# LoRA forward on one core: 12 projecting matmuls of 512 columns for 24 of 256, and a spread in two instructions a quadrant

## The chip, the cores and the metric

The kernel runs on one core of a Trainium2 chip. A core has five engines with instruction streams of their own: TensorE (PE, matmuls; its weight loads are shown apart as PEld), VectorE (DVE), ScalarE (ACT), GpSimd (POOL) and SyncE (SP), which issues the transfers here. Sixteen DMA engines move data between the chip's memory and the core's SBUF. Matmuls write into PSUM, a second memory. Engines order their work by semaphores. The metric is the time of one execution on the device, in microseconds (us); the kernel before takes 123.55 us (median of three runs, 123.49 to 123.74).

## The reference

```python
x      # 16 x 512 x 768, float32: 8192 tokens of 768
A      # 768 x 16;  B: 16 x 768;  scale = 0.5
lora = np.matmul(np.matmul(x, A), B)
return (x + scale * lora).astype(np.float32)
```

Every token is projected from 768 values to 16 (y = x A), raised back to 768 (y B), halved and added to x. x and the result are 25 MB each.

## The kernel before

**Tiles and groups.** The 8192 tokens are 64 tiles of 128 tokens, one token a partition. They lie in five parts of 9, 7, 16, 16 and 16 tiles (PARTS). SBUF holds 48 tiles of x as float32 (x_sb); the last part takes the place of the first two, once those are stored. Work goes in 8 groups of 8 tiles (GROUP); a group is raised and summed in four pairs of tiles.

**One group, step by step.**

1. Narrowing (L194): ScalarE copies the first four tiles and GpSimd the last four from x_sb (float32) to xn (float16). For groups after the first they wait for s_taken, which says that the projection of the group before has started and xn is free.
2. Turning (L250): VectorE transposes xn into xt in blocks of 32 x 32. It takes pairs of float16 values for one float32, so a block turns 32 tokens against 32 pairs. In xt a partition holds, for its quadrant of 32 tokens, one pair of columns of x out of each of 12 stretches of 64 columns (NC = 12); the two halves of a pair lie next to each other along the free axis (index k).
3. Projecting (L281): 24 matmuls of 256 columns (8 tiles x 32 tokens), one for each stretch c and half k, add up in ps_yt. The moving operand takes every second float16 of xt. The stationary operand w_bd[:, c, k, :] is block diagonal: quadrant b of the partitions holds the 32 rows of A of that stretch and half, in columns 32 b to 32 b + 15; the other 16 columns of each quadrant are zero. The last of the 24 raises s_y.
4. Spreading (L238): four instructions of ScalarE, one a quadrant, scale ps_yt by 0.5 and write it as float16 to the diagonal blocks of y_bd. What lies off the diagonal was set to zero once. The fourth raises s_spread.
5. Raising (L302): for each pair, four matmuls (512, 256, 256 and 512 columns) of y_bd with b_mm into one of two PSUM buffers (lora_ps). b_mm holds B four times, 32 partitions apart, with zeros in the other rows.
6. Summing (L255): VectorE adds lora_ps to x_sb, in place, one instruction a pair.

**The order of the work.** It is written out by hand for each engine. TensorE, for each group: raise pairs 0 and 1, wait for the next group's turning, the first half of its projection, raise pairs 2 and 3, the second half of the projection. Pair 0 waits for s_spread, each pair for a free buffer (s_free). VectorE: turn group g + 1, then sum the four pairs of group g. ScalarE: narrow group g + 1, then spread group g.

**The transfers.** All are issued by SP in one order: loads of the first two parts with A and B between, the loads of parts 2 and 3, stores 0 and 1 (16 tiles in all), loads 6 and 7 (8 tiles each, into the place of what was stored, each after one of these stores has landed), and stores 2, 3 and 4 (16 tiles each). A store waits for the sums of its tiles (s_sum). Two have one more gate: stores 0 and 1 wait for s_lora (L169), the second raised pair of group 2, and store 2 waits for s_raise (L181), the first raising matmul of group 5.

**At the start.** GpSimd sets a_rows, b_rows, pick, w_bd and y_bd to zero, makes pick (ones where a row of B goes), copies A into w_one and from there into the four quadrants of w_bd (L220); two matmuls of pick with b_half (L315) put B into its rows, and ScalarE copies that to b_mm (L231).

Of the kernel before, what the change touches and what calls it, by code (L numbers as in the profile page):

```python
# [9 lines left out]
MM_DT = mybir.dt.float16  # L10
# [6 lines left out]
GROUP = 8  # L17
# [6 lines left out]
APART = 4  # L24
# [4 lines left out]
def kernel(  # L29
# [9 lines left out]
    fp32 = mybir.dt.float32  # L39
    P = 128  # L40
    Q = 32
    NQ = P // Q
# [2 lines left out]
    out2 = out.flatten_outer_dims()  # L45
    T, D = x2.shape
    R = A.shape[1]
    NC = D // 64
    NG = sum(PARTS) // GROUP
    PAIRS = GROUP // 2  # L50
    assert sum(PARTS) * P == T and NG * GROUP == sum(PARTS)
    sc = float(scale)


    def sb(name, shape, dtype):
        return nc.alloc_sbuf_tensor(name, shape, dtype).ap()

    def ps(name, shape):
        return nc.alloc_psum_tensor(name, shape, fp32).ap()
# [4 lines left out]

    a_rows = sb("a_rows", [P, 64 * R], fp32)
    a_t = sb("a_t", [P, 2, R, Q], fp32)
    w_one = sb("w_one", [Q, NC, 2, R], MM_DT)
    b_rows = sb("b_rows", [P, D], fp32)  # L70
    b_half = sb("b_half", [P, D], MM_DT)
    pick = sb("pick", [P, NQ, Q], MM_DT)
    w_bd = sb("w_bd", [P, NC, 2, P], MM_DT)
    b_mm = sb("b_mm", [P, D], MM_DT)
    xn = sb("xn", [P, GROUP, D], MM_DT)
    xt = sb("xt", [P, GROUP, D], MM_DT)
    y_bd = sb("y_bd", [P, GROUP, P], MM_DT)
    lora = [ps(f"lora_ps{i}", [P, 2, D]) for i in range(2)]
    y_ps = ps("ps_yt", [P, GROUP, Q])

    sems = []

    def sem(name):
        sems.append(nc.alloc_semaphore(name))
        return sems[-1]
# [14 lines left out]
    def held(i, s, n):  # L100
        return tiles(where.index((i, s)), n)
# [12 lines left out]

    assert SETS * SET == NC
    s_a, s_b = sem("s_a"), sem("s_b")
    s_ready, s_brows, s_pick = sem("s_ready"), sem("s_brows"), sem("s_pick")
    s_w, s_bh, s_bp, s_bm = sem("s_w"), sem("s_bh"), sem("s_bp"), sem("s_bm")
    s_first, s_narrow, s_turned, s_taken = sem("s_first"), sem("s_narrow"), sem("s_turned"), sem("s_taken")
    s_y, s_spread, s_lora = sem("s_y"), sem("s_spread"), sem("s_lora")  # L120

    s_free = [sem(f"s_free{p}") for p in range(PAIRS)]
    s_out0, s_out1, s_raise = sem("s_out0"), sem("s_out1"), sem("s_raise")

    s_sum, s_out = sem("s_sum"), sem("s_out")

    MMS = 2 * NC
    STORES = [(0, 0, 9), (1, 0, 7), (2, 0, 16), (3, 0, 16), (4, 0, 16)]

    STORED = [where.index((i, s + n - 1)) // GROUP for i, s, n in STORES]  # L130
# [5 lines left out]
    def on_sync(e):  # L136
        def load(k):
            ld = LOADS[k]
            e.dma_start(out=held(*ld), in_=memory(x2, *ld)).then_inc(s_load[k], 16)  # L139

        def summed(k):
            e.wait_ge(s_sum, sorted(set(STORED)).index(STORED[k]) + 1)
            if STORED[k] + 1 < NG:

                e.sem_inc(s_free[PAIRS - 1], 1)

        def store(k, done):
            st = STORES[k]
            e.dma_start(out=memory(out2, *st), in_=held(*st)).then_inc(done, 16)

        load(0)
        load(1)
        e.wait_ge(s_ready, 1)
        blocks = A.rearrange("(c e) r -> c (e r)", e=64)
        for c in range(SETS):
            e.dma_start(
                out=a_rows[c : SET * SET : SET, :], in_=blocks[ds(c * SET, SET), :]
            ).then_inc(s_a, 16)
        e.wait_ge(s_brows, 1)
        e.dma_start(out=b_rows[0 : R * APART : APART, :], in_=B).then_inc(s_b, 16)  # L160
        for k in range(2, len(LOADS) - 2):
            load(k)

        for p in range(2, PAIRS):
            e.sem_inc(s_free[p], 1)
        summed(0)


        e.wait_ge(s_lora, 2 * PAIRS + 2)  # L169
        store(0, s_out0)  # L170
        store(1, s_out1)
        e.wait_ge(s_out0, 16)
        load(len(LOADS) - 2)
        e.wait_ge(s_out1, 16)
        load(len(LOADS) - 1)
        for k in range(2, len(STORES)):
            summed(k)
            if k == 2:


                e.wait_ge(s_raise, 6)  # L181
            store(k, s_out)

    here = set()
# [13 lines left out]
    def on_gpsimd(e):  # L198
        e.memset(a_rows[0:Q], 0.0).then_inc(s_ready, 1)  # L199
        e.memset(b_rows, 0.0).then_inc(s_brows, 1)  # L200
        e.memset(pick, 0.0).then_inc(s_pick, 1)
        e.memset(w_bd.rearrange("p c k m -> p (c k m)").bitcast(fp32), 0.0)  # L202
        e.memset(y_bd.rearrange("p s m -> p (s m)").bitcast(fp32), 0.0).then_inc(s_ready, 1)  # L203
        e.wait_ge(s_pick, 1)
        e.affine_select(  # L205
            out=pick, in_=pick, compare_op=mybir.AluOpType.not_equal, fill=1.0, base=0,
            pattern=[[0, NQ], [-APART, Q]], channel_multiplier=1,
        ).then_inc(s_pick, 1)
        narrowed(e, e.tensor_copy, 0, 0, SUB // 2)
        e.wait_ge(s_pick, 2)  # L210
        e.wait_ge(s_b, 16)
        e.tensor_copy(out=b_half, in_=b_rows).then_inc(s_bh, 1)  # L212
        e.wait_ge(s_ready, 3)
        e.tensor_copy(  # L214
            out=w_one.rearrange("i (c e) k r -> i c e (k r)", c=SETS),
            in_=a_t[0:Q].rearrange("i k r (e c) -> i c e (k r)", c=SET)[:, 0:SETS, 0:SET, :],
        ).then_inc(s_w, 1)
        e.wait_ge(s_w, 1)
        for b in range(NQ):
            e.tensor_copy(  # L220
                out=w_bd[ds(b * Q, Q), :, :, ds(b * Q, R)], in_=w_one
            ).then_inc(s_w, 1)
            e.wait_ge(s_w, b + 2)
        for g in range(1, NG):
            narrowed(e, e.tensor_copy, g, SUB)

    def on_scalar(e):
        narrowed(e, e.copy, 0, SUB // 2, SUB // 2)
        narrowed(e, e.copy, 0, SUB)
        e.wait_ge(s_bp, 1)  # L230
        e.copy(out=b_mm, in_=lora[0][:, 0, :]).then_inc(s_bm, 1)  # L231
        for g in range(NG):
            if g + 1 < NG:
                narrowed(e, e.copy, g + 1, 0)
            e.wait_ge(s_y, g + 1)
            for b in range(NQ):
                q = ds(b * Q, Q)
                last = e.mul(out=y_bd[q, :, q], in_=y_ps[q, :, :], mul=sc)  # L238
            last.then_inc(s_spread, 1)

    def on_vector(e):
        e.wait_ge(s_a, SETS * 16 + 1)
        e.transpose(  # L243
            out=a_t[0:Q].rearrange("i k r c -> i (k r) c"),
            in_=a_rows[0:Q].rearrange("c (i k r) -> c (k r) i", k=2, r=R),
        ).then_inc(s_ready, 1)
# [26 lines left out]
    def on_tensor(e):  # L273


        xv = xt.rearrange("p s (c j k) -> p s c j k", c=NC, k=2)

        def projected(first, last):
            for m in range(first, last):
                c, k = divmod(m, 2)  # L280
                mm = e.matmul(  # L281
                    y_ps, w_bd[:, c, k, :], xv[:, :, c, :, k],
                    start=(m == 0), stop=(m == MMS - 1),
                )
                if m == 0:
                    mm.then_inc(s_turned, -1)
                if m == 1:

                    mm.then_inc(s_taken, 1)
                if m == MMS - 1:  # L290
                    mm.then_inc(s_y, 1)

        def raised(p):
            if p == 0:
                e.wait_ge(s_spread, 1)
            free = s_free[(p + 2) % PAIRS]
            e.wait_ge(free, 1)
            t = lora[p % 2]
            mms = []
            for k in range(2):  # L300
                for n0, w in ((0, 512), (512, 256)) if k == 0 else ((0, 256), (256, 512)):
                    mms.append(e.matmul(  # L302
                        t[:, k, ds(n0, w)], y_bd[:, 2 * p + k, :], b_mm[:, ds(n0, w)],
                        start=True, stop=True,
                    ))
            if p == 0:
                mms[0].then_inc(s_raise, 1)
                mms[2].then_inc(s_spread, -1)
            mms[1].then_inc(free, -1)
            mms[-1].then_inc(s_lora, 1)  # L310

        e.wait_ge(s_pick, 2)
        e.wait_ge(s_bh, 1)
        for n0, w in ((0, 512), (512, 256)):
            last = e.matmul(  # L315
                lora[0][:, 0, ds(n0, w)], pick.rearrange("p b r -> p (b r)"),
                b_half[:, ds(n0, w)], start=True, stop=True,
            )
        last.then_inc(s_bp, 1)
        e.wait_ge(s_w, 1 + NQ)  # L320
        e.wait_ge(s_turned, 1)
        projected(0, MMS)
        e.wait_ge(s_bm, 1)
        with e.Fori(0, NG - 1):
            raised(0)
            raised(1)
            e.wait_ge(s_turned, 1)
            projected(0, MMS // 2)
            raised(2)
            raised(3)  # L330
            projected(MMS // 2, MMS)
        for p in range(PAIRS):
            raised(p)
# [50 lines left out]
```

## Time and profile before

| what | us |
|---|---|
| median of three runs (lowest, highest) | 123.55 (123.49, 123.74) |
| the profiled execution: its own time | 123.43 |
| its span, first to last instruction | 121.6 |
| busy: DVE, PE, ACT, POOL | 81.7, 49.8, 37.4, 28.4 |
| moved by DMA | 50.43 MB, mean 415 GB/s |
| DMA packets' time, share of 16 engines' span | 97.0% |

The span is what the profile's times are counted in; 1.83 us of that execution lie around it. A busy share is a mean over the whole span and says little about one stage. The views used are: the busy line and the 40 slices, the stretches (busy time of each engine between two moments), each engine's instructions in order of time (start, length, engine, line, operation, output from input, count, and in brackets the idle time before and what ended it), and the mean times of groups of instructions. SPq stands for the transfers that SP issues; the length of such a line runs from the first issue to the last. The trace also holds every DMA packet with its start, length and size.

### The profile page before, as it was taken

To read this page: it belongs to the slowest core of one execution; us is meant where nothing else is said; L and a number is where in the kernel's file an instruction comes from. 1 tells how busy PE (TensorE), PEld (TensorE's weight loads), DVE (VectorE), ACT (ScalarE), POOL (GpSimd) and SP (SyncE) were. 2 spreads that over 40 slices of the span, in tenths; PEclk is the share of its full clock that TensorE was granted. 3 is DMA by queue.
4 is the path that set the end of the run, shared out by engine and by line. 5 is a ranking of instruction groups with operands and counts; after the bars stand their busy time and mean duration, and the time that the engine had idled before them with its cause. 6 is when DMAs were issued, how large, how long until landed. Compare 5 with 4: busy or idle time off the path is not lost.

```text
span 121.6 us, 884 instructions
## 1 busy us (share of the span) xinstructions
PE 49.8 (41%) x322; PEld 29.2 (24%) x322; DVE 81.7 (67%) x42; ACT 37.4 (31%) x43; POOL 28.4 (23%) x24
## 2 busy tenths in 40 slices
PE   0000209487457547746745734774674320000000
PEld 0000006253223424424423322442442110000000
DVE  0000970599999999999999989999995990000000
ACT  4000967626408312735340093643004000000000
POOL 7730567126009002605300080620000000000000
PEclk9999999999999999999999999999999995555555
DMA  3999999999999897999999999998999899899890
GB/s 63 437 431 457 446 398 469 404 420 469 437 517 420 356 517 336 427 421 410 446 416 436 428 428 485 420 517 372 404 517 404 372 517 404 372 517 404 372 517 0
DMA packets 1928, 50.43 MB, mean 415 GB/s; under 512 B 236, under 2 KB 236, under 8 KB 392
## 3 DMA queue, kind: packets, MB, share of 16 engines
q1 hardware_dynamic: 1928, 50.43, 97.0%
HBM read 25.26 MB, written 25.17 MB: 415 GB/s over the span
## 4 chain that ended last, share of the span: by engine, by line
DVE 33%; DMA 29%; PE 9%; ACT 6%; POOL 2%; issue 2%; SPq 0%; DVEq 0%
DVE x_sb L255 21%; DMA x_sb<-in_x_dram 20%; DVE xt L250 12%; DMA out_dram<-x_sb 9%; PE ps_yt L281 6%; ACT xn L194 3%; PE lora_ps L302 3%; ACT y_bd L238 2%; POOL xn L194 2%; SPq L139 0%; SPq L379 0%; DVEq L268 0%; SPq L134 0%
## 5 line engine op out<-in xcount | busy, mean ns | idle before, releaser
L255 DVE TENSOR_TENSOR x_sb<-x_sb,lora_ps 128x1536 f32<-128x1536 f32 x32 | 53.7, 1735 | 1.4 <-PE lora_ps L302 1.4
L194 ACT CAST xn<-x_sb 128x3072 f16<-128x3072 f32 (+1 forms) x9 | 23.4, 2609 | 35.9 <-DMA x_sb<-in_x_dram 24.8
L302 PE MATMUL lora_ps<-b_mm,y_bd 128*128 128x512 f16 (+1 forms) x128 | 25.0, 328 | 22.6 <-ACT y_bd L238 14.3
L194 POOL CAST xn<-x_sb 128x3072 f16<-128x3072 f32 (+1 forms) x8 | 20.7, 2586 | 43.9 <-DMA x_sb<-in_x_dram 24.6
L250 DVE STREAM_TRANSPOSE xt<-xn 128x3072 f32<-128x3072 f32 (+1 forms) x9 | 27.1, 3006 | 5.3 <-PE ps_yt L281 4.4
L281 PE MATMUL ps_yt<-xt,w_bd 128*128 128x256 f16 x192 | 25.2, 282 | 12.2 <-DVE xt L250 12.2
L281 PEld LDWEIGHTS ps_yt<-xt,w_bd 128*128 128x128 f16 x192 | 18.5, 99 | 19.7 <-issue 15.4
L302 PEld LDWEIGHTS lora_ps<-b_mm,y_bd 128*128 128x128 f16 x128 | 10.6, 97 | 35.5 <-ACT y_bd L238 16.6
L238 ACT ACTIVATE y_bd<-ps_yt 32x256 f16<-32x256 f32 x32 | 12.0, 374 | 18.7 <-PE ps_yt L281 18.4
L243 DVE STREAM_TRANSPOSE a_t<-a_rows 32x1024 f32<-32x1024 f32 x1 | 2.0, 1955 | 12.2 <-DMA a_rows<-in_A_dram 12.2
L315 PE MATMUL lora_ps<-b_half,pick 128*128 128x512 f16 (+1 forms) x2 | 0.8, 500 | 13.5 <-POOL b_half L212 13.5
L315 PEld LDWEIGHTS lora_ps<-b_half,pick 128*128 128x128 f16 x2 | 0.1, 105 | 13.5 <-issue 13.5
L212 POOL CAST b_half<-b_rows 128x768 f16<-128x768 f32 x1 | 0.8, 827 | 5.5 <-DMA b_rows<-in_B_dram 5.5
L220 POOL COPY w_bd<-w_one 32x384 f16<-32x384 f16 x4 | 2.0, 500 | 0.2
L194 ACT ACT_TABLE_LOAD x1 | 1.3, 1283 | 0.9 <-SPq L134 0.9
L202 POOL MEMSET w_bd<- 128x1536 f32 x1 | 1.4, 1372 | 0.0
L214 POOL CAST w_one<-a_t 32x384 f16<-32x384 f32 x1 | 0.9, 857 | 0.9 <-DVE a_t L243 0.9
L199 POOL MEMSET a_rows<- 32x1024 f32 x1 | 0.9, 941 | 0.5 <-SPq L134 0.5
L231 ACT CAST b_mm<-lora_ps 128x768 f16<-128x768 f32 x1 | 0.8, 798 | 0.0
L200 POOL MEMSET b_rows<- 128x768 f32 x1 | 0.7, 728 | 0.0
L203 POOL MEMSET y_bd<- 128x512 f32 x1 | 0.5, 514 | 0.0
L205 POOL TENSOR_SCALAR_AFFINE_SELECT pick<-pick 128x128 f16<-128x128 f16 x1 | 0.3, 298 | 0.0
(5 smaller groups left out, 0.6 us busy)
## 6 DMA issues: line engine op xcount, KB each, us to landing
out_dram<-x_sb SPq DMA_DIRECT2D x3, 6144.0 KB, 20.1
x_sb<-in_x_dram SPq DMA_DIRECT2D x4, 3072.0 KB, 17.6
x_sb<-in_x_dram SPq DMA_DIRECT2D x1, 6144.0 KB, 41.6
x_sb<-in_x_dram SPq DMA_DIRECT2D x2, 2688.0 KB, 12.4
out_dram<-x_sb SPq DMA_DIRECT2D x1, 3456.0 KB, 11.5
out_dram<-x_sb SPq DMA_DIRECT2D x1, 2688.0 KB, 17.7
x_sb<-in_x_dram SPq DMA_DIRECT2D x1, 768.0 KB, 4.5
a_rows<-in_A_dram SPq DMA_DIRECT2D x3, 16.0 KB
```

What stands on the lines that cost most here:

```text
L194: ins = copy(out=xn[:, ds(first, n), :], in_=tiles(t, n))
L199: e.memset(a_rows[0:Q], 0.0).then_inc(s_ready, 1)
L202: e.memset(w_bd.rearrange("p c k m -> p (c k m)").bitcast(fp32), 0.0)
L214: e.tensor_copy(out=w_one.rearrange("i (c e) k r -> i c e (k r)", c=SETS), in_=a_t[0:Q].rearrange("i k r (e c) -> i c e (k r)", c=SET)[:, ...
L220: e.tensor_copy(out=w_bd[ds(b * Q, Q), :, :, ds(b * Q, R)], in_=w_one).then_inc(s_w, 1)
L238: last = e.mul(out=y_bd[q, :, q], in_=y_ps[q, :, :], mul=sc)
L243: e.transpose(out=a_t[0:Q].rearrange("i k r c -> i (k r) c"), in_=a_rows[0:Q].rearrange("c (i k r) -> c (k r) i", k=2, r=R),).then_inc(s_r ...
L250: return e.transpose(out=ts[0], in_=ts[1])
L255: ins = e.tensor_tensor(out=xs, in0=xs, in1=lora[p % 2], op=mybir.AluOpType.add)
L281: mm = e.matmul(y_ps, w_bd[:, c, k, :], xv[:, :, c, :, k], start=(m == 0), stop=(m == MMS - 1),)
L302: mms.append(e.matmul(t[:, k, ds(n0, w)], y_bd[:, 2 * p + k, :], b_mm[:, ds(n0, w)], start=True, stop=True,))
L315: last = e.matmul(lora[0][:, 0, ds(n0, w)], pick.rearrange("p b r -> p (b r)"), b_half[:, ds(n0, w)], start=True, stop=True,)
```

## The change

TensorE takes both halves of a pair in one matmul. The moving operand is a whole stretch of xt, 8 tiles x 32 tokens x 2 halves = 512 columns without a step; the stationary operand holds in each quadrant 32 columns, the 16 of A's rows for half 0 and beside them the 16 for half 1. There are 12 matmuls a group. The product has four parts for each quadrant, half of the weights by half of the columns, of which two are wanted: weights 0 with column 0 and weights 1 with column 1. ps_yt becomes 512 float32 a partition.

ScalarE picks the wanted ones. Four instructions read every second column (half 1) on 32 partitions and write the diagonal blocks of y_bd; in the lower 16 partitions of each quadrant what they write is not wanted. Then ScalarE waits for its own s_lower, and four more read the other columns (half 0) on the lower 16 partitions of each quadrant and write over it. The two halves of y then stand in 32 rows, B stands twice in each quadrant of b_mm (pick has eight blocks of 16 in place of four of 32), and the raising matmuls add the halves.

The gates move: stores 0 and 1 wait for s_most >= 3 and store 2 for s_most >= 6; s_most is raised by the second of the second four instructions of each group. The semaphore s_raise goes.

```diff
-    MMS = 2 * NC
+    MMS = NC
-    pick = sb("pick", [P, NQ, Q], MM_DT)
-    w_bd = sb("w_bd", [P, NC, 2, P], MM_DT)
+    pick = sb("pick", [P, 2 * NQ, R], MM_DT)
+    w_bd = sb("w_bd", [P, NC, P], MM_DT)
-    y_ps = ps("ps_yt", [P, GROUP, Q])
+    y_ps = ps("ps_yt", [P, GROUP, Q, 2])
...
-        e.wait_ge(s_lora, 2 * PAIRS + 2)
+        e.wait_ge(s_most, 3)
         store(0, s_out0)
...
-                e.wait_ge(s_raise, 6)
+                e.wait_ge(s_most, 6)
             store(k, s_out)
...
-            pattern=[[0, NQ], [-APART, Q]], channel_multiplier=1,
+            pattern=[[0, 2 * NQ], [-APART, R]], channel_multiplier=1,
...
             e.tensor_copy(
-                out=w_bd[ds(b * Q, Q), :, :, ds(b * Q, R)], in_=w_one
+                out=w_bd[ds(b * Q, Q), :, ds(b * Q, Q)],
+                in_=w_one.rearrange("i c k r -> i c (k r)"),
             ).then_inc(s_w, 1)
...
             for b in range(NQ):
                 q = ds(b * Q, Q)
-                last = e.mul(out=y_bd[q, :, q], in_=y_ps[q, :, :], mul=sc)
+                last = e.mul(out=y_bd[q, :, q], in_=y_ps[q, :, :, 1], mul=sc)
+            last.then_inc(s_lower, 1)
+
+            e.wait_ge(s_lower, g + 1)
+            for b in range(NQ):
+                last = e.mul(
+                    out=y_bd[ds(b * Q, R), :, ds(b * Q, Q)], in_=y_ps[ds(b * Q, R), :, :, 0], mul=sc
+                )
+                if b == 1:
+                    last.then_inc(s_most, 1)
             last.then_inc(s_spread, 1)
...
-        xv = xt.rearrange("p s (c j k) -> p s c j k", c=NC, k=2)
+        xv = xt.rearrange("p s (c i) -> p s c i", c=NC)
...
-                c, k = divmod(m, 2)
                 mm = e.matmul(
-                    y_ps, w_bd[:, c, k, :], xv[:, :, c, :, k],
+                    y_ps.rearrange("p s j k -> p s (j k)"), w_bd[:, m, :], xv[:, :, m, :],
                     start=(m == 0), stop=(m == MMS - 1),
                 )
...
             if p == 0:
-                mms[0].then_inc(s_raise, 1)
                 mms[2].then_inc(s_spread, -1)
```

More of the change, by code (lines that the diff above doesn't have):

```diff
@@ L47 @@
     R = A.shape[1]
+    assert 2 * R == Q
     NC = D // 64
@@ L119 @@
     s_first, s_narrow, s_turned, s_taken = sem("s_first"), sem("s_narrow"), sem("s_turned"), sem("s_taken")
-    s_y, s_spread, s_lora = sem("s_y"), sem("s_spread"), sem("s_lora")
+    s_y, s_lower, s_spread, s_lora = sem("s_y"), sem("s_lower"), sem("s_spread"), sem("s_lora")
     s_free = [sem(f"s_free{p}") for p in range(PAIRS)]
-    s_out0, s_out1, s_raise = sem("s_out0"), sem("s_out1"), sem("s_raise")
+    s_out0, s_out1, s_most = sem("s_out0"), sem("s_out1"), sem("s_most")
     s_sum, s_out = sem("s_sum"), sem("s_out")
-    MMS = 2 * NC
+    MMS = NC
     STORES = [(0, 0, 9), (1, 0, 7), (2, 0, 16), (3, 0, 16), (4, 0, 16)]
@@ L201, in on_gpsimd @@
         e.memset(pick, 0.0).then_inc(s_pick, 1)
-        e.memset(w_bd.rearrange("p c k m -> p (c k m)").bitcast(fp32), 0.0)
+        e.memset(w_bd.rearrange("p c m -> p (c m)").bitcast(fp32), 0.0)
         e.memset(y_bd.rearrange("p s m -> p (s m)").bitcast(fp32), 0.0).then_inc(s_ready, 1)
@@ L315, in on_tensor @@
             last = e.matmul(
-                lora[0][:, 0, ds(n0, w)], pick.rearrange("p b r -> p (b r)"),
+                lora[0][:, 0, ds(n0, w)], pick.rearrange("p h r -> p (h r)"),
                 b_half[:, ds(n0, w)], start=True, stop=True,
```

## The prediction

> **What bounds the kernel now.** I read the page's busy line, slices and queue part first. No compute engine is above 67% (DVE), while the DMA row stands at 9 or close to it from the second slice to the second last.
>
> ```profile
> PE 49.8 (41%) x322; PEld 29.2 (24%) x322; DVE 81.7 (67%) x42; ACT 37.4 (31%) x43; POOL 28.4 (23%) x24
> ...
> DMA  3999999999999897999999999998999899899890
> ...
> q1 hardware_dynamic: 1928, 50.43, 97.0%
> ```
>
> Then the same by stretches (per line: width, busy time of PE, PEld, DVE, ACT, POOL, clock, DMA share, GB/s). The share is 0.97 to 1.02 from 12 to 101 us whatever the engines do, at 415 to 439 GB/s; 50.43 MB at 434 GB/s are 116.2 us of the 121.6.
>
> ```profile
> 18.00:26.00 8.00, 5.74 (x32) 3.61 (x32) 3.55 (x3) 4.25 (x5) 2.74 (x1) 1.00 1.02 439
> 26.00:44.40 18.40, 11.88 (x80) 7.09 (x80) 18.40 (x10) 8.50 (x10) 5.49 (x2) 1.00 1.01 434
> ...
> 70.00:101.00 31.00, 16.10 (x106) 9.09 (x104) 28.86 (x16) 9.68 (x14) 5.21 (x2) 0.98 1.00 434
> ```
>
> So what counts is whether the queue ever runs dry, and that is read from SP's issues:
>
> ```profile
> 4.57 2.08 SPq L139 DMA_DIRECT2D x_sb<-in_x_dram  x4
> 44.45 0.82 SPq L149 DMA_DIRECT2D out_dram<-x_sb  x2
> 55.95 6.91 SPq L139 DMA_DIRECT2D x_sb<-in_x_dram  x2
> 74.47 26.50 SPq L149 DMA_DIRECT2D out_dram<-x_sb  x3
> ```
>
> I set these against the trace's single DMA packets (start, length, size). The queue is served in the order of issue, and every one of the 16 DMA engines has its next packet directly behind the last, from 2.0 us to 119.2 (the earliest engine) or 120.2 (the latest). A transfer therefore delays the end only if it is issued after the latest engine has run dry. First packets, earliest to latest engine: stores 0 and 1 46.47 to 47.29, issued 44.45; store 2 75.70 to 76.51, issued 74.47; store 4 104.7 to 105.7, issued 100.64 (a store of 16 tiles is 8 packets of 1.815 us an engine, back to back). Store 3, issued 82.67, is needed at 90. From issue to first packet: load 0, on an empty queue, took 1.0 us (0.97 to 1.98); store 2 took 1.23 with no gap in front of it, so it needs no more than that. I take 1.23. Spare time, with that taken off: 1.6 us at store 0 and 3.8 at store 4 for the latest engine. At store 2 it is 0.4, since the engine that ends last (120.23) begins store 2 at 76.09 and loses time later; the one that begins it at 76.51 ends at 120.02.
>
> The loop behind it is paced by VectorE, and ScalarE's spread is in its other branch:
>
> ```profile
> 41.36 1.53 ACT L238 ACTIVATE y_bd<-ps_yt 32x256 f16<-32x256 f32 x4 [2.18 <-PE ps_yt L281]
> ...
> 72.46 1.53 ACT L238 ACTIVATE y_bd<-ps_yt 32x256 f16<-32x256 f32 x4
> ...
> 91.42 1.53 ACT L238 ACTIVATE y_bd<-ps_yt 32x256 f16<-32x256 f32 x4 [8.38 <-PE ps_yt L281]
> ```
>
> ```profile
> 42.36 3.36 DVE L250 STREAM_TRANSPOSE xt<-xn 128x3072 f32<-128x3072 f32 x1
> 45.65 6.71 DVE L255 TENSOR_TENSOR x_sb<-x_sb,lora_ps 128x1536 f32<-128x1536 f32 x4
> ...
> 93.86 6.75 DVE L255 TENSOR_TENSOR x_sb<-x_sb,lora_ps 128x1536 f32<-128x1536 f32 x4 [1.37 <-PE lora_ps L302]
> ```
>
> A group takes VectorE 9.92 us without a gap (one transpose, four sums). Its first sum needs the spread and four raising matmuls: y is done at 41.34 in group 2, sums begin at 45.65, so that branch has 4.3 us and uses about 2.5 (1.54 of spread, 0.06 to PE, 0.82 of raising, 0.04 to VectorE).
>
> **The change part by part.**
>
> *TensorE.* The columns stay: 24 x 256 = 12 x 512 = 6144 a group. The last 12 before y take 1.50 us now: 11 steps of 0.112 and a last one of 0.27. A 512-column step, from the raising matmuls (8 in 1.47 us, 3072 columns, last one 0.38: 1.09 for 2560), is 0.218. Six: 5 x 0.218 + 0.38 = 1.47, a gain of 0.03. The first group's 24 took 4.26, the early ones slower (415 ns each against 271). Bounds for the 12: all at the warm step 2.8, all at twice that 5.2; it is the same columns through the same start-up, so 4.3. I book nothing. Had it 5.2, everything below moves 0.9 later in the first half, inside the 1.6 at store 0.
>
> *ScalarE.* Before, four instructions of 0.374, stepping by 0.385. After: eight, and between the fours ScalarE waits for its own semaphore. GpSimd's copies into w_bd have such a wait (2.18 us for four of 0.500: 0.06 each). Spread = 8 x 0.385 + 0.06 = 3.14, against 1.54: +1.6 a group, 12.8 us in all on an engine busy 37 of 121.6. Both instructions have 256 elements a partition as now; only the reads step by two words in PSUM. No row of the kernel before shows ScalarE reading so. Lower bound 0.374, for there are no fewer elements. Upper bound: the two strided reads that the trace has. GpSimd's w_one took 857 ns for 384 elements; contiguous casts there give 187 + 0.833 an element (827 for 768, 2746 for 3072), so 1.75 an element, 2.1 times. VectorE's a_t took 1955 for 1024; its transposes give 135 + 1.05 (1750, 3365), so 1.78, 1.7 times. ScalarE itself: 374 for 256 and 798 for 768 elements out of PSUM, so 162 + 0.83; twice the element price is 586. Both strided rows step 128 bytes, out of SBUF; this one steps 8 bytes in PSUM on ScalarE, nearest to y_bd's own row. I take 0.374 and keep 0.586.
>
> What waits for it: in the first group raising starts at 24.10 + 1.6 = 25.7, its four matmuls end 26.5, and the first sum starts 26.55 in place of 25.87: everything in the loop 0.7 later. From then on the branch takes 0.03 + 3.14 + 0.06 + 0.82 + 0.04 = 4.1 of the 4.3, 0.2 spare, so nothing adds up; the next projection and the copies of the following group follow 0.7 later too. At group 5 load 6's copies on ScalarE end at 72.43 as now (the landing is the DMA's); spread 72.46 to 75.6, sums from 76.5 in place of 75.9: again 0.6 to 0.7 late. The last group has no transpose to hide it: y at 91.4 + 0.65 = 92.05, sums from 96.15 (now 93.86), their end 102.9, store 4 issued 102.9, first packets at most 104.15 against 105.7 for the latest engine. 1.5 us spare are left: booked at nothing. Without that cover each us late would be a us of time.
>
> *The gates on SP.* Stores 0 and 1 wait for half of the second four of group 2, no longer for its second raise: 41.36 + 0.7 + 6 x 0.385 + 0.06 + 0.03 = 44.45, as now. Store 2 waits for the same point of group 5, not for its first raised matmul: 72.46 + 2.31 + 0.06 + 0.03 = 74.86, 0.4 later; first packets by 76.09 at 1.23, by 75.86 at load 0's 1.0. The engine that ends last wants them at 76.09: 0 to 0.2 us spare, the tightest place of all. Engines that want them from 75.70 stand still for up to 0.4 us, but these end up to 1.0 us ahead of the last. Behind this wait on SP only stores 3 and 4 are queued. Booked at nothing.
>
> *The rest.* GpSimd's memset of w_bd halves (1.37 to about 0.73, from b_rows' 728 ns for 768); GpSimd then waits for load 0 until 5.57 anyway. The copies into w_bd keep 384 elements; they end at 17.35, and PE waits for VectorE until 18.1. pick, b_half and b_mm keep their sizes. [...]
>
> Sum against the profiled execution (123.43 us: its span of 121.6 and 1.83 around it): 0 + 0 + 0. That execution is 0.1 below the median of 123.55. I say 123.5.
>
> **The rivals.**
>
> *The strided read costs twice* (slower). At 0.586 the spread is 8 x 0.597 + 0.06 = 4.84, and the branch 5.8 of 4.3. First group +2.4, each further group +1.5. Group 2's gate falls at 48.85, first packets at 50.1 against 47.29: 2.8 us dry. Sums of the last group: 2.4 + 6 x 1.5 - 0.4 (VectorE's wait for load 6 that is there now) + 3.3 (no transpose hides it there) give 14.3 us later, so store 4 is issued near 114.9, first packet 116.2, 10.5 past 105.7: about 134 us. The point from which it adds up is 0.40 an instruction (4.3 us of branch); at 0.45 (branch 4.7) group 5's y comes 2.9 late at 74.0, its gate falls at 76.9, first packets 78.1, 2.0 dry: about 125.4. For it: both strided rows. Against: their step is 16 times as long. [...] No row of the kernel before decides. Chance 0.13, and 0.05 for a price between 0.40 and 0.5.
>
> *Store 2 comes late.* With a wait of ScalarE for itself of 0.3 us and more, or some tenths more from issue to packet, the engine that ends last runs dry. Price: what exceeds 1.23 us of latency and 0.06 of wait, say 0.3 to 0.8 us, so 123.8 to 124.3. Against: 0.06 in GpSimd's row, 1.23 with no gap. Chance 0.08.
>
> *A little faster.* The latest DMA engine is late through packets of up to 1.906 us in place of 1.815 between 76 and 100 us, while the compute engines run; after 103.9 it has none. If fewer instructions (96 matmuls and 96 weight loads less, 32 of ScalarE more) spare it these, the next engine ends the kernel, at 120.0 in place of 120.2: 123.3. That alone stays inside the bound. Another settling of the 16 engines in the first loads, where they lose 0.1 to 1.3 us each, could pass it. Chance of over 0.2%: 0.12.
>
> **How the numbers follow.** 0.2% (0.25 us) is about what a measurement of this kernel tells from no change. Hidden throughout: 0.62, with its own range 123.2 to 123.8. Slower: 0.13 + 0.05 + 0.08 = 0.26. Faster: 0.12. The range leaves out the doubled read (0.13) and little else: low 123.0, high 125.0.
>
> **What would show it.** Right: ScalarE's instructions at 372 to 376 ns for both shapes; spread 3.1 us; VectorE's groups still 9.9 us apart; store 2 issued near 74.9 and store 4 near 102.9; DMA share 1.00 from 70 to 101. Wrong: instructions above 400 ns, VectorE waiting for raised matmuls in every group, or a DMA share below 0.95 after 44 or after 74 us.

## The result, and the profile after

The changed kernel takes 125.32 us (median of six runs, 124.88 to 125.54) against 123.57 us (six runs, 123.44 to 123.74): 1.0136 times the time before, 95% interval 1.0115 to 1.0157. I had said 123.5 us, no change, with a range up to 125.0. The sign is that of the rivals, but by a cause that none of them named.

The profiled execution took 125.24 us, its span is 123.5. Its page (the busy line, and in 40 slices TensorE's clock and the DMA share):

```profile
span 123.5 us, 724 instructions
...
PE 60.5 (49%) x226; PEld 24.3 (20%) x226; DVE 82.4 (67%) x42; ACT 49.4 (40%) x75; POOL 27.8 (23%) x24
...
PEclk9999999995995897798599589779859955555555
DMA  3999999999989979999999989996996996999890
```

TensorE has 226 matmuls in place of 322 and is busy for 60.5 us in place of 49.8. The clock row points to a reason: from the tenth slice on it dips to half (5) again and again. In the kernel before, the same row is full until the last matmul:

```profile
PEclk9999999999999999999999999999999995555555
```

One group on TensorE, after (start, length, what; in brackets the wait before):

```profile
36.63 1.90 PE L314 MATMUL lora_ps<-b_mm,y_bd 128*128 128x512 f16 x8 [3.20 <-ACT y_bd L247]
38.37 2.71 PE L293 MATMUL ps_yt<-xt,w_bd 128*128 128x512 f16 x6
40.88 1.52 PE L314 MATMUL lora_ps<-b_mm,y_bd 128*128 128x512 f16 x8
42.24 1.46 PE L293 MATMUL ps_yt<-xt,w_bd 128*128 128x512 f16 x6
46.90 1.94 PE L314 MATMUL lora_ps<-b_mm,y_bd 128*128 128x512 f16 x8 [3.20 <-ACT y_bd L247]
```

The same in the kernel before:

```profile
42.95 1.47 PE L302 MATMUL lora_ps<-b_mm,y_bd 128*128 128x512 f16 x8 [1.62 <-ACT y_bd L238]
45.87 1.50 PE L281 MATMUL ps_yt<-xt,w_bd 128*128 128x256 f16 x12 [1.45 <-DVE xt L250]
```

After the change, the same six matmuls take 2.71 us in the first half of a projection and 1.46 in the second; the first raising takes 1.90, where it took 1.47. Once a group, after the wait of 3.20 us for the spread, a stretch runs at half clock. The trace has 15 changes of the clock between 27.29 and 98.97 us, each a whole number of 3.413 us after the first record at 23.87, and the view of stretches can be laid on these moments (width, busy time of PE, PEld, DVE, ACT, POOL, clock, DMA share, GB/s):

```profile
40.94:44.35 3.41, 2.76 (x15) 1.17 (x13) 3.17 (x3) 1.89 (x3) 1.33 (x1) 1.00 1.07 461
44.35:47.77 3.42, 0.87 (x5) 0.51 (x6) 3.42 (x2) 2.39 (x7) 0.00 (x0) 1.00 0.84 359
47.77:51.18 3.41, 3.41 (x10) 1.26 (x9) 3.41 (x3) 1.40 (x1) 1.35 (x1) 0.50 1.10 470
51.18:54.59 3.41, 2.77 (x15) 1.19 (x13) 3.14 (x3) 1.95 (x3) 1.40 (x1) 1.00 1.02 438
```

In the stretch that holds the wait, PE is busy for 0.87 us; the next one is granted half clock, and after that the clock is full again. The emptiest stretch inside the kernel before's loop is this, and the clock stayed full behind it:

```profile
41.72:45.13 3.41, 1.47 (x8) 0.70 (x8) 3.41 (x2) 1.14 (x4) 0.00 (x0) 1.00 1.03 447
```

VectorE and the stores, after:

```profile
45.10 3.37 DVE L263 STREAM_TRANSPOSE xt<-xn 128x3072 f32<-128x3072 f32 x1
48.40 3.38 DVE L268 TENSOR_TENSOR x_sb<-x_sb,lora_ps 128x1536 f32<-128x1536 f32 x2
52.04 3.42 DVE L268 TENSOR_TENSOR x_sb<-x_sb,lora_ps 128x1536 f32<-128x1536 f32 x2 [0.27 <-PE lora_ps L314]
55.38 3.37 DVE L263 STREAM_TRANSPOSE xt<-xn 128x3072 f32<-128x3072 f32 x1
...
99.07 6.75 DVE L268 TENSOR_TENSOR x_sb<-x_sb,lora_ps 128x1536 f32<-128x1536 f32 x4 [2.55 <-PE lora_ps L314]
```

```profile
46.09 0.82 SPq L153 DMA_DIRECT2D out_dram<-x_sb  x2
56.02 7.39 SPq L143 DMA_DIRECT2D x_sb<-in_x_dram  x2
76.87 29.31 SPq L153 DMA_DIRECT2D out_dram<-x_sb  x3
```

Groups are 10.28 us apart (45.10 to 55.38) in place of 9.92, and VectorE now waits for raised pairs inside a group. Stores 0 and 1 are issued at 46.09 (before: 44.45), store 2 at 76.87 (74.47), and the last sums end at 105.8 (100.6). In the packets the queue runs dry twice: an engine stands still for 0.23 us on average near 46.9 and for 0.62 near 77.7. The last packet ends at 122.15 us in place of 120.23, 1.92 later.

Followed engine by engine, these 1.92 us have two parts. 15 of the 16 engines stand still for 0.60 to 0.79 us before store 2, begin it at 77.71 to 77.85 (before: 75.70 to 76.51) and end at 121.37 to 121.66. Their end follows from the late issue of store 2. What they had lost earlier disappears in that wait: the gap near 46.9, and the last packets of store 1, which took 1.29 to 1.59 us where most of its packets take 0.80. The 16th engine has no gap there. It carried a packet of load 6 of 1.72 us in place of 0.91 at 62.7, and at 74.4 a packet of 8 KB of instructions (0.31 us) with one of 1.20 behind it; it ends load 7 at 78.64 and everything at 122.15. Without it, the last packet would have ended at 121.66, so about 1.4 us come from store 2 and 0.5 from this engine.

### The profile page after: what moved, and what is told of

It reads as the page before. It is cut to its first block, busy times and chain, and to the rows that moved or that the text cites. A ratio compares the mean times of both kernels' runs of the same rounds, so it can differ in the third digit from the quotient of the medians.

```text
span 123.5 us, 724 instructions
## 1 busy us (share of the span) xinstructions
PE 60.5 (49%) x226; PEld 24.3 (20%) x226; DVE 82.4 (67%) x42; ACT 49.4 (40%) x75; POOL 27.8 (23%) x24
## 4 chain that ended last, share of the span: by engine, by line
PE 45%; ACT 23%; DMA 8%; DVE 7%; issue 2%; SPq 0%
PE ps_yt L293 26%; PE lora_ps L314 19%; ACT y_bd L242 10%; ACT y_bd L247 10%; DMA x_sb<-in_x_dram 8%; DVE x_sb L268 5%; ACT xn L197 3%; DVE xt L263 1%; SPq L143 0%; SPq L390 0%; SPq L138 0%
## 5 line engine op out<-in xcount | busy, mean ns | idle before, releaser
L268 DVE TENSOR_TENSOR x_sb<-x_sb,lora_ps 128x1536 f32<-128x1536 f32 x32 | 54.4, 1741 | 5.6 <-PE lora_ps L314 5.6
L314 PE MATMUL lora_ps<-b_mm,y_bd 128*128 128x512 f16 (+1 forms) x128 | 29.1, 378 | 26.5 <-ACT y_bd L247 25.6
L293 PE MATMUL ps_yt<-xt,w_bd 128*128 128x512 f16 x96 | 34.4, 516 | 3.6 <-DVE xt L263 3.6
L314 PEld LDWEIGHTS lora_ps<-b_mm,y_bd 128*128 128x128 f16 x128 | 12.7, 109 | 43.6 <-ACT y_bd L247 30.0
L242 ACT ACTIVATE y_bd<-ps_yt 32x256 f16<-32x256 f32 x32 | 12.0, 374 | 16.9 <-PE ps_yt L293 16.6
L293 PEld LDWEIGHTS ps_yt<-xt,w_bd 128*128 128x128 f16 x96 | 11.5, 123 | 21.9 <-issue 17.6
L247 ACT ACTIVATE y_bd<-ps_yt 16x256 f16<-16x256 f32 x32 | 12.0, 374 | 0.6
L205 POOL MEMSET w_bd<- 128x768 f32 x1 | 0.7, 732 | 0.0
```

What stands on the lines that cost most here:

```text
L242: last = e.mul(out=y_bd[q, :, q], in_=y_ps[q, :, :, 1], mul=sc)
L247: last = e.mul(out=y_bd[ds(b * Q, R), :, ds(b * Q, Q)], in_=y_ps[ds(b * Q, R), :, :, 0], mul=sc)
L268: ins = e.tensor_tensor(out=xs, in0=xs, in1=lora[p % 2], op=mybir.AluOpType.add)
L293: mm = e.matmul(y_ps.rearrange("p s j k -> p s (j k)"), w_bd[:, m, :], xv[:, :, m, :], start=(m == 0), stop=(m == MMS - 1),)
L314: mms.append(e.matmul(t[:, k, ds(n0, w)], y_bd[:, 2 * p + k, :], b_mm[:, ds(n0, w)], start=True, stop=True,))
```

## The experiments

My theory after the result: **the clock**. The longer spread leaves TensorE idle for so long (3.20 us a group in place of 1.62) that its clock is halved, and matmuls at half clock make the loop longer than VectorE's 9.92 us, so that stores come late. The rivals: **length** (1.6 us more spread are too much for the branch at any clock), **form** (matmuls of 512 columns are slower by themselves) and **gates** (the new ones come too late).

**TensorE kept busy.** `busy` is a PSUM tile of 512 float32 a partition, the room of one result of 512 columns, that nobody reads:

```diff
             if p == 0:
+                for _ in range(8):
+                    e.matmul(busy, w_bd[:, 0, :], b_mm[:, 0:512], start=True, stop=True)
                 e.wait_ge(s_spread, 1)
```

> The changed kernel, and TensorE runs eight matmuls of 512 columns into an unused PSUM bank before it waits for each spread; nothing else moves. Theory (the clock): in the changed kernel TensorE waits 3.2 us for each spread, its clock is halved for one stretch of 3.41 us after that, and the matmuls at half clock stretch a group from 9.92 to 10.25 us; kept busy, it keeps its clock: mean clock above 0.90, groups 9.9 us apart, store 2 issued near 74.9, 123.5 us (123.2 to 123.8). Rival (length): the spread's 1.6 us more are too long for the branch at any clock: 125.3 or more, groups still 10.25. Rival (form): matmuls of 512 columns without a step are slower by themselves: 125.3.

Measured: 123.67 us, 1.0015 of before (1.0005 to 1.0026), mean clock of the profiled execution 0.910, as in the kernel before (the half clock behind the last matmul is in that mean). The stretches on the clock's moments, and the stores:

```profile
41.92:45.33 3.41, 1.93 (x10) 0.70 (x8) 3.41 (x2) 3.00 (x8) 0.00 (x0) 1.00 1.08 461
45.33:48.75 3.42, 3.33 (x18) 1.41 (x16) 3.42 (x3) 1.14 (x1) 1.11 (x1) 1.00 0.74 315
72.64:76.05 3.41, 1.36 (x8) 0.58 (x7) 3.41 (x2) 2.67 (x8) 0.00 (x0) 1.00 1.06 454
76.05:79.47 3.42, 3.42 (x11) 1.36 (x9) 3.10 (x3) 0.83 (x1) 0.78 (x1) 0.50 0.93 402
```

```profile
44.34 0.82 SPq L154 DMA_DIRECT2D out_dram<-x_sb  x2
55.76 6.98 SPq L144 DMA_DIRECT2D x_sb<-in_x_dram  x2
74.66 29.32 SPq L154 DMA_DIRECT2D out_dram<-x_sb  x3
```

With 1.93 us of work in it, the stretch of the spread is followed by full clock. Only group 5, whose spread waits for load 6's copies, falls to 1.36 and loses one stretch. Eight useless matmuls a group take 1.65 us off the kernel. Length, form and gates are all still there, so none of them alone is the cause.

**ScalarE's part alone**, on the kernel before:

```diff
                 last = e.mul(out=y_bd[q, :, q], in_=y_ps[q, :, :], mul=sc)
+            last.then_inc(s_lower, 1)
+            e.wait_ge(s_lower, g + 1)
+            for b in range(NQ):
+                q = ds(b * Q, Q)
+                last = e.mul(out=y_bd[q, :, q], in_=y_ps[q, :, :], mul=sc)
             last.then_inc(s_spread, 1)
```

> The kernel before with its 24 matmuls of 256 columns and its gates; ScalarE alone does more: it makes its four instructions a second time, with the same result, behind a wait for its own semaphore. Theory (the clock): TensorE's wait grows from 1.6 to 3.2 us, so the clock falls as in the changed kernel: mean clock near 0.80, groups 10.2 to 10.3 us apart, 124.8 to 125.8 us. Rival (length): also near 125.3, but at a clock near 0.91. Rival (form): 123.5, for the 512-column matmuls are not there. Rival (gates): 123.5.

Measured: 128.61 us, 1.0409 (1.0389 to 1.0430), clock 0.806. The clock falls with 256-column matmuls too, so form is not needed for it. The time is 3 us worse than I expected, and the lines say where:

```profile
46.96 2.74 PE L307 MATMUL lora_ps<-b_mm,y_bd 128*128 128x512 f16 x8 [3.19 <-ACT y_bd L243]
```

```profile
49.73 0.82 SPq L149 DMA_DIRECT2D out_dram<-x_sb  x2
```

The gate of stores 0 and 1 of the kernel before waits for this raising, which at half clock ends at 49.7. The DMA engines had run dry at 46.6 to 47.1 and stood still for 3.8 us on average; near 81 they did so again, for 0.75, since store 2 was issued only at 80.63. So the change's new gates, which wait for ScalarE, spared it this.

**TensorE's part alone**: the changed kernel without the second four.

```diff
-            last.then_inc(s_lower, 1)
-            e.wait_ge(s_lower, g + 1)
-            for b in range(NQ):
-                last = e.mul(
-                    out=y_bd[ds(b * Q, R), :, ds(b * Q, Q)], in_=y_ps[ds(b * Q, R), :, :, 0], mul=sc
-                )
                 if b == 1:
                     last.then_inc(s_most, 1)
```

> The changed kernel without ScalarE's second four instructions and the wait between: it leaves out the half of the projection that these pick, so half of A has no part in the output and what is not wanted stays in the lower rows; TensorE's 12 matmuls of 512 columns, the layout and the strided reads stay. Theory (the clock) and rival (length): TensorE waits 1.6 us as before, clock near 0.91, groups 9.9 us apart, 123.5 us (123.2 to 123.8). Rival (form): 125.3 with a low clock or long matmuls.

Measured: 123.77 us, 1.0019 (1.0005 to 1.0032), clock 0.907, groups 9.92 us apart up to the one that waits for load 6.

```profile
45.54 1.46 PE L286 MATMUL ps_yt<-xt,w_bd 128*128 128x512 f16 x6 [1.47 <-DVE xt L256]
```

The 512-column matmuls leave the clock and the loop as they were, so form is out. The 0.2% need not be theirs: the gate of stores 0 and 1 opens earlier here (42.21), and what that does is seen in the kernel before without gates, below.

**No gates.**

```diff
-        e.wait_ge(s_most, 3)
         store(0, s_out0)
...
-            if k == 2:
-                e.wait_ge(s_most, 6)
             store(k, s_out)
```

> The changed kernel without the two waits for s_most on SP: each store waits for its sums alone. Theory (the clock, and the loss reaches the end through late stores): clock stays near 0.80 and groups 10.25 us apart, but stores 0, 1 and 2 are queued long before the queue runs dry; then store 4, issued near 105.8 behind the late last sums, is the next that is late, and its first packet near 106.7 stands against 104.7 to 105.7 without any loss: about 124.4 (124.0 to 124.8). If the loss did not go through these stores at all: 125.3. If the last store is not late: 123.5.

Measured: 125.40 us, 1.0158 (1.0136 to 1.0179), clock 0.828: no gain, 1 us above what I expected, and the time that I had given for a loss that does not go through these stores. The lines show that it goes through the next one:

```profile
65.84 41.23 SPq L153 DMA_DIRECT2D out_dram<-x_sb  x3
```

```profile
99.96 6.75 DVE L264 TENSOR_TENSOR x_sb<-x_sb,lora_ps 128x1536 f32<-128x1536 f32 x4 [3.41 <-PE lora_ps L310]
```

Store 2 is issued at 65.84, and nothing is dry near 77. But the last sums end at 106.7, not 105.8, since in this execution the half clock fell on the first raising of each group; store 4's first packets are at 107.6, and the queue stands still for 1.25 us an engine at 106 to 108. Packets of loads 6 and 7 also rose to 977 ns on average, from 922 in the changed kernel. A slow loop has two ways into the time, the gate of store 2 and the sums before store 4, and in these two kernels they cost about the same.

**The kernel before without its gates** is the comparison for that:

> The kernel before without its two gates, so that each store waits for its sums alone; for comparison with the changed kernel without gates, which was no better than with them. If the gates only delay: 123.5. If a store queued behind loads that still run slows these (in the changed kernel without gates the packets of loads 6 and 7 took 977 ns in place of 922): 123.6 to 124.2, with the loads' packets above 930 ns against 915.

Measured: 123.94 us, 1.0043 (1.0029 to 1.0057). The gates are worth 0.4%. The packets of loads 6 and 7, which I had in mind, stay below 930 ns on average. Those of load 5 do not: the stores are issued at 43.20 in place of 44.45, and the last 16 packets of load 5, which start from 44.64 on, take 2.14 to 2.91 us in place of 1.82. TensorE's part alone, with the stores issued at 42.21, has the same (2.16 to 2.89); the kernel before, the changed kernel without gates (45.30) and the kernel with one more instruction (45.19, below) do not (1.82 to 1.87). Behind that the queue is never dry, and the last packet ends at 120.61 in place of 120.23. In this execution group 5's stretch held 0.77 us of matmuls and the next was at half clock, but no gap in the queue follows from it. Why the last packets of load 5 are longer in these two kernels stays open.

**How long may the wait be?** On the kernel before, one or two of the four spreading instructions are made again:

```diff
+            last.then_inc(s_lower, 1)
+            e.wait_ge(s_lower, g + 1)
+            for b in range(1):     # range(2) in the second run
+                q = ds(b * Q, Q)
+                last = e.mul(out=y_bd[q, :, q], in_=y_ps[q, :, :], mul=sc)
             last.then_inc(s_spread, 1)
```

> The kernel before, and ScalarE makes one of its four spreading instructions a second time behind a wait for its own semaphore: the spread takes 0.45 us more. The runs so far bear out the clock theory; this asks for its law. In them a stretch of 3.41 us in which TensorE multiplied for 0.35 of the time or less was followed by half clock (one exception), and one with 0.37 or more was not; the kernel before has many at 0.38. Theory (share of a stretch): TensorE waits 2.1 us, and the emptiest stretch holds this wait and one raising of two pairs, 1.28 us, which is 0.375: the clock holds, 123.3 to 123.8 us, clock near 0.91. Rival (the wait itself is what counts, and anything over the 1.6 us of before is too long): clock below 0.88 and over 124.

> The kernel before with two of the four spreading instructions made a second time: the spread takes 0.83 us more, the branch from y to the first sum 3.3 of its 4.3 us. Theory (share of a stretch): TensorE waits 2.45 us, so a stretch can fall to 0.28; the clock halves after some groups, not all, since the stretches slide against the groups: clock between 0.80 and 0.90, 124 to 127 us (with this kernel's gates, which wait for raised pairs). Rival (length of the branch alone): 3.3 is under 4.3, so 123.5.

Measured: one more, 1.0081 (1.0054 to 1.0109), clock 0.895; two more, 1.0128 (1.0108 to 1.0147). In the two kernels' profiles:

```profile
41.78:45.19 3.41, 1.47 (x8) 0.70 (x8) 3.41 (x2) 1.78 (x5) 0.00 (x0) 1.00 1.03 447
72.50:75.91 3.41, 1.12 (x8) 0.70 (x8) 2.91 (x2) 2.17 (x6) 0.42 (x1) 1.00 0.99 425
```

```profile
52.77:56.18 3.41, 0.99 (x9) 0.54 (x8) 3.41 (x3) 2.24 (x6) 0.00 (x0) 1.00 1.15 495
56.18:59.60 3.42, 3.42 (x16) 1.72 (x14) 3.42 (x3) 0.86 (x1) 0.83 (x1) 0.50 0.83 355
```

With one more, most stretches still hold 1.47 us and keep the clock, as the theory says. But my range made no allowance for those that don't: three runs took 123.85, 124.19 and 124.71 us, at mean clocks of 0.895, 0.883 and 0.871, and a fourth 126.30. The time is the one that I had given to the rival, but in the profile the clock stays full behind most waits of 2.03 us, which the rival excludes. With two more, stretches with 0.99 us lose the clock. (The second profile is of an execution of 127.44 us, longer than the kernel's others of 124.77 to 125.21; only its clock is read.) What costs these others their 1.3% is not shown. The branch has 1 us to spare (3.3 of 4.3), but three of the four had mean clocks of 0.897 to 0.899 at 125.00 to 125.21 us, and the one at 0.807 took 124.77: here the time does not follow the mean clock. The gates of the kernel before stand behind the spread, so the 0.83 us more also delay store 2, for which the prediction counts 0.4 us to spare (0.8 with the 0.85 us from issue to first packet that the changed kernel showed); that would be an estimated 0.03 to 0.4 of the 1.5 us, not all of it.

**Fewer filling matmuls**: three, and six, in place of eight.

> The changed kernel with three matmuls of 512 columns into the unused bank ahead of each wait for the spread, in place of eight. Theory (share of a stretch): they leave a wait of 2.55 us, so a stretch can fall to 0.25, and the clock still halves after some groups: clock between 0.80 and 0.90, 123.9 to 125.3 us. Rival (any matmul in the wait is enough): 123.6 with a clock near 0.91.

> The changed kernel with six matmuls of 512 columns in the wait for each spread (eight kept the clock, three did not). Theory (a stretch of 3.41 us needs between 0.35 and 0.37 of multiplying): they leave a wait of 1.9 us, and the emptiest stretch holds one raising of two pairs, 0.375: the clock holds but for the group that waits for load 6, 123.4 to 123.9 us, clock 0.87 to 0.92. If the law were a longest wait near 1.6 us: the clock halves in most groups, below 0.87, over 124.

Measured: with three 123.96 us, 1.0046 (1.0017 to 1.0075), the clock of the runs 0.82 to 0.85: five of them took 123.50 to 123.74 us and five 124.19 to 124.94, at clocks that overlap (0.839 to 0.853 and 0.817 to 0.841), so a lower clock alone does not settle the time; with six 123.59 us, 0.9998 (0.9979 to 1.0017), clock 0.90 in the profile. Six matmuls are enough, and with them the changed kernel is as fast as the kernel before.

**Could the order do without filling?** TensorE's second half of the projection goes ahead of raising pair 3, with two buffers for y_bd. It was run with the loop over the groups written out, and again as a loop.

```diff
-            raised(2)
-            raised(3)
+            raised(2, g)
             projected(MMS // 2, MMS)
+            raised(3, g)
```

> The changed kernel with TensorE's order turned: the second half of the projection goes ahead of the raising of pair 3, so y is done about 1.6 us earlier in each group and pair 3 is raised while ScalarE spreads. Two buffers for y_bd are needed for it, and the loop over the groups is written out. No filling matmuls. Theory (the clock hurts only where the branch has no slack left): TensorE still waits some 2.5 us for a spread, so the clock still halves after some groups (0.80 to 0.90), but raised pair 0 is ready before VectorE's transpose ends even at half clock: groups 9.9 us apart, 123.3 to 123.9 us. Rival (half clock costs the time by itself, wherever it falls): 124.5 to 125.5. Better than the kernel before by over 0.2%: not expected, for its queue has no gap to close.

> As the run with the early y, but the loop over the groups is kept as a loop (two groups a turn, since y_bd has two buffers). With the loop written out, groups were 9.9 us apart and the clock mostly held, and still 125.2 us: one DMA engine ended 0.9 us after all others, having carried two packets of 16 KB of the instruction queue, at 53 and at 99 us, with its own packets beside them up to 2.4 us long. Theory (the early y mends the loop; what was lost there came from instructions fetched for the longer program): no instruction packets of 16 KB, groups 9.9 us apart, 123.4 to 124.0 us. Rival (the early y does not mend the changed kernel): 124.8 or more without such packets.

Measured: 1.0120 (1.0073 to 1.0166), with three runs of 125.07 to 125.26 us and one of 127.84; and 1.0175 (1.0134 to 1.0216), with four runs of 124.38 to 125.78 and two of 126.57 and 127.74. The second interval reaches past 2%, so whether that is slower or the same is unclear. The loop is mostly mended in both profiles: behind the first group, groups are 9.92 us apart, but for 11.48 at group 5 of the first; store 2 is issued at 75.66 and 74.83. The time is not, and my expectation for the second was wrong. What its profile shows is in the queue part:

```profile
q1 hardware_dynamic: 1928, 50.43, 96.2%
q8 instruction: 1, 0.02, 0.0%
q14 instruction: 1, 0.01, 0.0%
```

Two packets of instructions came through the data's DMA engines. The one of 16 KB, at 92.7 us, took 0.93 us, and the packets around it 2.40 and 2.20 in place of 1.82: 1.9 us on one engine, which ended at 121.25, while the other 15 ended between 119.4 and 120.7; the one at 120.7 had carried a packet of 8 KB at 72.9. Without these two engines the last packet would end at 120.0. That accounts for the profiled execution of 124.38 us; runs of 125.6 and 125.8 had no profile, and what they lost stays open.

No version was faster than the kernel before.

## Why the prediction was wrong

- **The bound** (a queue that is full from 2 to 120 us, and late issues as the only way into the time) held for 15 of the 16 DMA engines, and the tightest place, store 2, was the right one. The engine that ended last had another way into the time: long packets and one of instructions, worth 0.5 of the 1.92 us. From issue to first packet I took 1.23 us; behind an empty queue it was 0.85 (46.09 to 46.94, 76.87 to 77.71).
- **ScalarE** was right. The strided reads cost nothing: 374 ns for both kinds, as without a step before, and a spread of 3.1 us. The rival that priced them at 586 falls.

```profile
L242 ACT ACTIVATE y_bd<-ps_yt 32x256 f16<-32x256 f32 x32 | 12.0, 374 | 16.9 <-PE ps_yt L293 16.6
L247 ACT ACTIVATE y_bd<-ps_yt 16x256 f16<-16x256 f32 x32 | 12.0, 374 | 0.6
```

- **TensorE: this is the step that failed.** "I book nothing" was worked out with matmuls at full clock, 0.218 a step of 512 columns, and the branch with 0.82 for a raising. Half of them took much longer: six in 2.6 to 2.8 us against 1.47, the raising of two pairs 1.9 to 2.0 against 1.47. The first 12, priced 4.3, took 5.28, the upper bound: the trace's first record of full clock is at 23.9 us, behind them, in place of 21.2 (the clock row counts the time ahead of that record as full). The stretches in the prediction show the clock (1.00, 0.98) and its sum takes it as a property of the kernel, while in the runs it went with the very waits that the change lengthens: a mean clock of 0.804 with waits of 3.20 us, and of 0.910 with eight matmuls in them. The sum has each raising wait 1.6 us longer for the spread, and never asks what an idle TensorE does.
- **"0.2 spare, so nothing adds up"** failed with it. The loop closed on another chain: raising 1.90, half a projection 2.55, raising 1.32, half 1.31, spread with its hand-overs 3.19 (from 36.63 to 46.90), 10.27 us, over VectorE's 9.92. At full clock I estimate the same chain, from the half and the raising that ran at full clock, at 1.3 + 1.3 + 1.3 + 1.3 + 3.2 = 8.4.
- **The gates**: 44.45 and 74.86 were predicted, 46.09 and 76.87 came, each late by what the loop had lost. With TensorE kept busy they fell at 44.34 and 74.66, so the working was right but for the clock. Store 4 was predicted at 102.9 and issued at 105.85.
- **The rivals**: "store 2 comes late" named the place, with another cause and a third of the price. "A little faster" did not show: one engine is again 0.5 us behind the others at the end, by other packets than before.

In these runs a wait shorter than 3.20 us was enough, and the stretch ahead of half clock was not empty: half clock came behind most waits of 2.41 us with two more spreading instructions, behind all eight of 2.42 to 2.56 with three filling matmuls, and behind stretches that were busy for up to 0.41.

What remains open: why store 1's last packets, at 60 to 62 us, are long on all 16 engines in the changed kernel (up to 1.59 us) and on a few in the kernel before. On 15 engines they cost nothing, since these then waited for store 2; what they cost the 16th is not known.

## What to carry to other kernels

Here idle time of TensorE had a price, though VectorE had paced the loop: a wait of 3.20 us a group in place of 1.62 took the mean clock to 0.804 and the time to 1.0136. So before lengthening a wait of TensorE, lay the profile's stretches on the moments at which the clock changes and see how much work the emptiest one keeps. A few matmuls into an unused PSUM tile bought the clock back here: six a group, 0.9998. And where a queue is full to the last tenth, look for every place at which a slower loop reaches it: without the gates store 2 was no longer late, store 4 was, and the time stayed at 125.40 us.

## What the runs showed of the hardware

- **In these runs the clock went with the share of work in a stretch.** In the 13 profiled executions there are 251 stretches of 3.413 us at full clock between 17 and 108 us. PE's busy time, from the records as the profile counts it, was at most 0.41 of the stretch in 61, and all 61 were followed by half clock; it was 0.43 or more in 190, and none of these was. In my expectations I counted columns instead and found exceptions; with the busy time of the records there are none. The emptiest stretches in the kernel before's loop hold 1.47 of 3.413 us, 0.43: just above the fullest that half clock followed, and one more instruction on ScalarE (0.45 us with its wait), inside the time that the branch had to spare, cost it 0.8%.
- **Packets of instructions fell between the data's packets.** In the changed kernel one engine's data stop at 74.40 us and go on at 74.70, with the packet of instructions exactly between. A packet of 8 KB took 0.31 us and the one behind it 0.3 to 0.4 longer (the changed kernel at 74.4 us, with eight filling matmuls at 70.8); one of 16 KB cost its engine 1.9 us (the early y as a loop, at 92.7). In the changed kernel it was the engine that ended last, at 122.15 us against 121.37 to 121.66 for the others.
- **ScalarE's spreading instructions** took 374 ns for 256 elements a partition in all three forms here: on 32 partitions without a step (L238 of the kernel before), and with every second word of PSUM on 32 and on 16 partitions (L242 and L247 of the changed kernel).
